# A hybrid encoder layer in fp32r: four more pairs of up tiles by seven products, their weight sums made in DRAM

## The chip, the cores and the metric

The kernel runs on one core of a Trainium2 chip. The metric is device time in microseconds (us). TensorE is called PE (its weight loads PEld), VectorE DVE, ScalarE ACT, GpSimd POOL, and SyncE SP, which issues most of the transfers.

## The reference

One layer on x (512 tokens by 1024 channels, float32) and a memory of 256 tokens:

```python
h = rmsnorm(x, norm_mix)
(fq, fk, fv, ff, gq, gk, gv, gb, ga, gz, sq, sk, sv, gates) = split_projection(h @ w_in)
ya = fox_attention(...)            # 4 heads, softmax with a forgetting gate
yb = gated_delta_rule(...)         # 4 heads, chunked recurrence
yc = stick_breaking_attention(...) # 4 heads, blocks of 128 queries, strict causal mask
mixed = g0 * (ya @ w_oa) + g1 * (yb @ w_ob) + g2 * (yc @ w_oc)
x = x + mixed @ w_out
x = x + memory_cross_attention(rmsnorm(x, norm_xq), rmsnorm(mem, norm_mem), w_mq, w_mkv, ..., w_mo)
x = x + conv_ffn(rmsnorm(x, norm_ffn), w_up, ffn_conv, ffn_conv_b, w_down)

def conv_ffn(h, w_up, conv_w, conv_b, w_down):
    u = causal_dwconv(h @ w_up, conv_w) + conv_b
    a, b = jnp.split(u, 2, axis=-1)
    return (jax.nn.silu(a) * b) @ w_down
```

w_up is 1024 by 5632, w_down 2816 by 1024. The last line of the layer, the gated MLP, is what the change is about.

## The kernel before, in words

Everything lies with channels on the 128 partitions and the 512 tokens along the row. Weights come in units of 128 x 1024 float32 (512 KB): eight blocks of 128 x 128. A matrix product is kept exact enough by splitting each float32 operand into a high part, rounded to the matmul's type fp32r, and a low part, the rest; a block then takes three matmuls: high by high, weight's high by the tokens' low, and weight's low by the tokens' high. `mm3` puts the 16 matmuls with the weight's high part first (L212, L213) and the 8 with its low part behind (L215).

A unit is loaded by SP into one of three raw tiles (`wraw`, L178), its high part copied by ACT (`whi`, L186), its low part subtracted by DVE (`wlo`, L187). `split_adding` makes the low part without DVE: ACT writes the negated, rounded weights into `alo` (L292), and a DMA issued by POOL adds the raw weights from DRAM to it (L293).

The program runs in stages: three mixers with their gates, in an order written out by hand (`ORDER`: a letter for a step, a number for a head or half); the output projection; the cross-attention; the up products, and the down products. Each engine then works through its own instructions in the order that the program and its scheduler gave it; a wait at the head of an engine's queue holds everything behind it. POOL has little to do: in each of the four stick-breaking heads (`s0` to `s3`) it writes the causal mask into score tiles (AFFINE_SELECT at L846 and L858), and later it issues the `alo` transfers. DVE and ACT wait for these masks, and the stick head is interleaved with the gate products on PE.

The up stage has 22 pairs m of tiles (tile m and tile m + 22: the two inputs of the gate). Three kinds of pairs:

- raw pairs (m below `RAW_UP`): the products start from the un-normalised tokens `xf`, while the root of the mean square, `r_f`, is still being made (`xfps`, `rfa`, `rfb`, L1050 to L1061); the results are multiplied by `r_f` (L1191);
- plain pairs: 48 matmuls of 512 columns on the normalised tokens `xn`, made by `up_norm` (L1078 to L1080);
- seven-product pairs (m in `SEVEN`): the pair of units and the tokens' halves taken as a 2 by 2 block product in seven half products instead of eight (`seven`, 84 matmuls of 256 columns). They need four sums of weight blocks a pair (s1 to s4, DVE, L305 to L315) and sums of the tokens, made once (`token_forms`).

`gated` then runs the convolution, the silu and the product, and gives `hid`. The down stage takes 12 of the 22 hidden tiles by seven products too (`seven_down`, with sums of four weight blocks a unit by DVE at L1247 to L1249) and the others plainly, in two halves of four output tiles.

Of the kernel before, what the change touches and what calls it, by code (L numbers as in the profile page):

```python
# [16 lines left out]
P = 128  # L17
# [5 lines left out]
SPARE = 2  # L23
JS = (5, 6, 7, 8, 9, 10)
FORM_SLOTS = 8
AHEAD = 4
ADD_A22 = True
ADD_PLAIN = (0, 1)
# [53 lines left out]
def build(nc, tc, ctx, x_t, mem_t, w, cols_d, const_d, unit_d, out_t, dbg=None):  # L82
# [9 lines left out]
    def tiles_of(which, tag, bufs, shape=(T,)):  # L92
# [19 lines left out]
    ahead = tiles_of("ahead", "a", AHEAD, (1024,))  # L112
# [5 lines left out]
    spilled = ctx.enter_context(tc.tile_pool(name="spill", bufs=1, space=bass.MemoryType.DRAM)).tile(  # L118
        [P, KC, T], F32, tag="x3", name="x3_spill")
# [54 lines left out]
    last_mm = []  # L174

    def load_unit(u):
        raw = wp.tile([P, 1024], F32, tag="wraw", name=f"wraw{u}", bufs=WB[0])
        nc.sync.dma_start(raw, w[u])  # L178
        return raw
# [101 lines left out]
    def sums_of_tokens(e, o, f):  # L281


        V.tensor_tensor(e[:, LEFT], e[:, RIGHT], e[:, LEFT], ALU.subtract)
        V.tensor_tensor(two(f), two(e), o[:, None, RIGHT].to_broadcast([P, 2, T // 2]), ALU.add)
        V.tensor_tensor(e[:, RIGHT], f[:, LEFT], o[:, LEFT], ALU.subtract)

    def split_adding(u, src, cols, name):

        lo = ahead(f"alo{name}", F32R)[:, :cols.stop - cols.start]  # L290
        hi = wp.tile([P, 1024], F32R, tag="whi", name=f"whi{name}", bufs=WB[1])[:, :cols.stop - cols.start]
        S.activation(lo, src, AF.Copy, scale=-1.0)  # L292
        G.dma_start(lo, w[u, :, cols], accum_op=ALU.add)  # L293
# [3 lines left out]
    def seven(u, name, xs, forms, sums, outs, rest):  # L297


        a1, a2 = load_unit(u), load_unit(u + 1)  # L300
        (a11, a12), (a21, a22) = [(t[:, :T], t[:, T:]) for t in (a1, a2)]

        h1, l1 = split_adding(u, a1, slice(0, 2 * T), f"{u}")
        s1, s2, f12 = sums("12")
        V.tensor_tensor(s1, a21, a22, ALU.subtract)  # L305
        V.tensor_tensor(s2, a11, s1, ALU.subtract)
        w5, w6 = f12()
        if ADD_A22:
            h2, l2 = split_adding(u + 1, a22, slice(T, 2 * T), f"{u + 1}")
        else:  # L310
            h2, l2 = (wp.tile([P, 1024], F32R, tag=t, name=f"{t}{u + 1}", bufs=b) for t, b in (("whi", WB[1]), ("wlo", WB[2])))
            split_blocks(a22, h2[:, :T], l2[:, :T])
# [1109 lines left out]
```

## Time and profile before

| | |
|---|---|
| median of 3 runs | 1044.39 us (1044.11 to 1044.57) |
| profiled execution's own time | 1044.74 us |
| its span | 1043.0 us |
| busy: PE, DVE, ACT, POOL | 1029.4, 748.8, 602.8, 58.1 us |
| moved by DMA | 115.06 MB, of it 14.42 MB by POOL's accumulates |
| up stage on PE | from 691.28 to about 923.4 us |
| granted TensorE clock | 1.00 |

A row of a timeline gives the start and length in us, engine, line, operation, output tile <- input tiles; a bracket tells how long the engine had been idle and what ended that. PE's instructions overlap a little, so the distance between starts (0.23 us for 512 columns, 0.12 for 256), not the length of one, is what a matmul costs.

### The profile page before, as it was taken

To read this page: it belongs to the slowest core of one execution; us is meant where nothing else is said; L and a number is where in the kernel's file an instruction comes from. 1 tells how busy PE (TensorE), PEld (TensorE's weight loads), DVE (VectorE), ACT (ScalarE), POOL (GpSimd) and SP (SyncE) were. 2 spreads that over 40 slices of the span, in tenths; PEclk is the share of its full clock that TensorE was granted. 3 is DMA by queue.
4 is the path that set the end of the run, shared out by engine and by line. 5 is a ranking of instruction groups with operands and counts; after the bars stand their busy time and mean duration, and the time that the engine had idled before them with its cause. 6 is when DMAs were issued, how large, how long until landed. Compare 5 with 4: busy or idle time off the path is not lost.

```text
span 1043.0 us, 14582 instructions
## 1 busy us (share of the span) xinstructions
PE 1029.4 (99%) x5529; PEld 873.1 (84%) x5529; DVE 748.8 (72%) x1262; ACT 602.8 (58%) x986; POOL 58.1 (6%) x116
## 2 busy tenths in 40 slices
PE   9999999999999999999999999999999999999998
PEld 7778888778888888788887888778889999989997
DVE  6697768788455443457657757679889988999873
ACT  6376757646242644654545657655677777855431
POOL 0000000101010000000000000000111111100000
PEclk9999999999999999999999999999999999999999
DMA  6323221111211111222434323142777788732441
GB/s 235 101 81 101 76 67 61 72 61 63 80 61 62 59 43 61 81 81 81 153 123 127 122 86 119 43 158 96 188 179 185 178 194 191 173 101 103 161 143 61
DMA packets 34342, 115.06 MB, mean 110 GB/s; under 512 B 3936, under 2 KB 4192, under 8 KB 33760
## 3 DMA queue, kind: packets, MB, share of 16 engines
q1 hardware_dynamic: 29088, 99.45, 28.3%
q0 software_dynamic: 4896, 14.42, 8.4%
q8 instruction: 43, 0.70, 0.3%
q10 hardware_dynamic: 288, 0.27, 0.1%
q14 instruction: 27, 0.22, 0.1%
HBM read 109.93 MB, written 4.19 MB: 109 GB/s over the span
## 4 chain that ended last, share of the span: by engine, by line
PE 94%; DVE 2%; ACT 1%; DMA 1%; issue 1%; SPq 0%; POOL 0%; ACTq 0%; DVEq 0%; POOLq 0%
PE dn L1221 8%; PE g L212 4%; PE g L213 4%; PE g L215 4%; PE up L215 3%; PE up L213 3%; PE up L212 3%; PE px L267 2%; PE px L269 2%; PE gk L469 2%; PE px L266 2%; PE dz L1221 2%; PE dx L1221 2%; PE f L212 1%; PE s L213 1%; PE s L215 1%
## 5 line engine op out<-in xcount | busy, mean ns | idle before, releaser
L186 ACT ACTIVATE whi<-wraw 128x1024 fp32r<-128x1024 f32 x117 | 123.8, 1058 | 150.4 <-PE g L213 38.7
L187 DVE TENSOR_TENSOR wlo<-wraw,whi 128x1024 fp32r<-128x1024 f32 x117 | 142.7, 1220 | 42.7 <-ACT whi L186 21.4
L212 PE MATMUL g<-hh,whi 128*128 128x512 f32 x192 | 77.5, 404 | 1.6 <-DVE gate L485 1.6
L213 PE MATMUL g<-hl,whi 128*128 128x512 f32 x192 | 75.8, 395 | 0.0
L293 POOL DMA_DIRECT2D alo<-w x34 | 29.5, 866 | 422.2 <-ACT alo L292 419.8
L215 PE MATMUL g<-hh,wlo 128*128 128x512 f32 x192 | 51.5, 400 | 0.0
L1221 PE MATMUL dn<-room,whi 128*128 128x256 f32 (+1 forms) x176 | 49.6, 333 | 0.0
L1118 DVE SCALAR_TENSOR_TENSOR uc<-u,cols,uc 128x511 f32<-128x511 f32 (+1 forms) x68 | 48.5, 749 | 0.7 <-ACT uc L1116 0.7
L212 PEld LDWEIGHTS g<-hh,whi 128*128 128x128 f32 x192 | 36.2, 188 | 10.8 <-DVE gate L485 1.4
L215 PEld LDWEIGHTS g<-hh,wlo 128*128 128x128 f32 x192 | 35.8, 188 | 8.3 <-issue 0.5
L213 PEld LDWEIGHTS g<-hl,whi 128*128 128x128 f32 x192 | 36.2, 188 | 7.7
L294 ACT ACTIVATE whi<-wraw 128x1024 fp32r<-128x1024 f32 (+1 forms) x34 | 30.3, 892 | 15.9 <-PE py L267 8.8
L485 DVE TENSOR_TENSOR gate<-g,r_x 128x512 f32<-128x512 f32 x24 | 16.4, 688 | 30.8 <-PE g L215 30.8
L292 ACT ACTIVATE alo<-wraw 128x1024 fp32r<-128x1024 f32 (+1 forms) x34 | 30.2, 887 | 13.1 <-DMA wraw<-w 12.1
L274 DVE TENSOR_TENSOR sl<-s,sh 128x1024 fp32r<-128x1024 f32 x26 | 31.8, 1223 | 5.2 <-ACT sh L273 5.1
L1221 PE MATMUL dn<-room,wlo 128*128 128x512 f32 (+1 forms) x128 | 34.0, 352 | 0.0
L1221 PEld LDWEIGHTS dn<-room,whi 128*128 128x128 f32 x176 | 29.8, 188 | 3.4
L212 PE MATMUL up<-xnh,whi 128*128 128x512 f32 x80 | 31.6, 395 | 0.0
L1221 PE MATMUL dn<-hidl,whi 128*128 128x512 f32 x80 | 31.6, 395 | 0.0
L213 PE MATMUL up<-xnl,whi 128*128 128x512 f32 x80 | 31.6, 395 | 0.0
L273 ACT ACTIVATE sh<-s 128x1024 fp32r<-128x1024 f32 x26 | 27.3, 1051 | 5.6 <-PE px L267 3.2
L1116 ACT ACTIVATE uc<-u,cols 128x512 f32<-128x512 f32 x34 | 26.7, 809 | 4.5 <-DVE u L1191 3.6
(991 smaller groups left out, 3094.4 us busy)
## 6 DMA issues: line engine op xcount, KB each, us to landing
wraw<-w SPq DMA_DIRECT2D x166, 512.0 KB, 3.5
alo<-w POOLq DMA_DIRECT2D x21, 512.0 KB, 6.4
alo<-w POOLq DMA_DIRECT2D x13, 256.0 KB, 5.8
x<-x_t SPq DMA_DIRECT2D x8, 256.0 KB, 6.7
xr<-x_t SPq DMA_DIRECT2D x2, 1024.0 KB, 5.9
x_spill<-xr SPq DMA_DIRECT2D x2, 1024.0 KB, 4.3
x<-x_spill SPq DMA_DIRECT2D x8, 256.0 KB, 4.1
mem_sb<-mem_t SPq DMA_DIRECT2D x4, 256.0 KB, 4.7
```

The costliest lines, as they stand in the source:

```text
L186: S.activation(hi, raw, AF.Copy)
L187: V.tensor_tensor(lo, raw, hi.bitcast(F32), ALU.subtract)
L212: PE.matmul(ps, hi[:, b], xh, start=first and i == 0, stop=False)
L213: PE.matmul(ps, hi[:, b], xl, start=False, stop=False)
L215: mm = PE.matmul(ps, lo[:, b], xh, start=False, stop=last and i == len(xs) - 1)
L273: S.activation(hi, src, AF.Copy)
L274: V.tensor_tensor(lo, src, hi.bitcast(F32), ALU.subtract)
L292: S.activation(lo, src, AF.Copy, scale=-1.0)
L293: G.dma_start(lo, w[u, :, cols], accum_op=ALU.add)
L294: S.activation(hi, src, AF.Copy)
L1118: V.scalar_tensor_tensor(c[:, s:], u[:, :T - s], col("ffn_conv", 3 * j + 2 - s), c[:, s:], ALU.mult, ALU.add)
L1221: mm = PE.matmul(ps[:, z], lhs, rhs, start=first is None, stop=last, skip_group_check=True)
```

## The change

`SEVEN` grows from 13 pairs to 17 (m = 5 to 21), `RAW_UP` from 4 to 5 (m = 0 to 4), so no normalised plain pair is left. Norms and token forms are made between the raw pairs (`TOKENS`), in place. All ten raw units use `split_adding`, with their low parts in tiles of the pool "hidden" (tags `wsh`, `wsl`); before, the raw units were split by DVE, and `alo` lay in a pool of its own ("ahead").

The sums of weights aren't made by DVE any more. For each seven-product pair SP copies two units within DRAM, and POOL issues three accumulating DMAs from DRAM to DRAM, one for a step of the program (`sums_of_weights`; 512 KB, 256 KB, 256 KB); for each three units of the down stage two copies and four accumulates (`sums_of_down`). `advance_sums` runs one step of every open job after the steps named in `SUMS_AFTER`, from `A0` on; POOL's DMAs are pinned in program order. `seven` and `seven_down` load the finished sums through SP and split them. The signs of the seven products change with that, the low parts of seven-product units are split by DVE, and the down stage's first half runs its plain blocks with the hidden tile outside and both pairs of outputs within each group of units.

```diff
+SUMS_AFTER = {s: 1 for s in "A0 C0 n0 S1 S2 s1 s2 n1 z n2 n3 S3 s3 a0 y0 A1 a1 B0 c0 y1 y2 C1 c1".split()}
+ADD_RAW = (0, 1)
-RAW_UP = 4
-FORMS = 4
-NORMS = {0: 2, 1: 6}
-SEVEN = (7, 8, 9, 10, 11, 12, 13, 14, 16, 17, 18, 19, 20)
-SPLITS = {18: 10}
+RAW_UP = 5
+FORMS = 3
+TOKENS = {0: "n0 n4 f0", 1: "n1 n5 f1", 2: "n2 n6 f2", 3: "n3 n7 f3"}
+SEVEN = (5, 6, 7, 8, 9, 10, 11, 12, 13, 14, 15, 16, 17, 18, 19, 20, 21)
+SPLITS = {18: 3, 19: 2, 20: 2}
...
-    def split_adding(u, src, cols, name):
-
-        lo = ahead(f"alo{name}", F32R)[:, :cols.stop - cols.start]
...
+    def split_adding(src, dram, name, alloc):
+
+        lo = alloc(f"alo{name}", F32R)
+        hi = wp.tile([P, 1024], F32R, tag="whi", name=f"whi{name}", bufs=WB[1])
         S.activation(lo, src, AF.Copy, scale=-1.0)
-        G.dma_start(lo, w[u, :, cols], accum_op=ALU.add)
+        G.dma_start(lo, dram, accum_op=ALU.add)
         S.activation(hi, src, AF.Copy)
         return hi, lo
...
+    def sums_of_weights(m):
+
+        u = UNITS["up"] + 2 * m
+        t = dram.tile([P, 2048], F32, tag=f"sums{m}", name=f"sums{m}")
+        s31, s2, s4 = t[:, :1024], t[:, 1024:1536], t[:, 1536:]
+        summed[m] = t
+        with tc.issue_after(last_load[0]):
+            nc.sync.dma_start(s31, w[u + 1])
+            nc.sync.dma_start(t[:, 1024:], w[u])
+        yield
+        pin(G.dma_start(s31.rearrange("p (a b) -> p a b", a=2), w[u:u + 2, :, :T].rearrange("a p b -> p a b"), accum_op=ALU.add))
+        yield
+        pin(G.dma_start(s2, s31[:, T:], accum_op=ALU.add))
+        yield
+        pin(G.dma_start(s4, s2, accum_op=ALU.add))
...
+    def advance_sums(n):
+
+        for s in list(steps):
+            if next(s, steps) is steps:
+                steps.remove(s)
+        for _ in range(n):
+            job = next(jobs, None)
+            if job is not None:
+                steps.append(job)
+                next(job)
...
+        h1, l1 = load("1", w[u])
+        hs31, ls31 = load("3", sums[:, :1024])
+        h2, l2 = load("2", w[u + 1, :, T:])
+        hs24, ls24 = load("4", sums[:, 1024:])
...
+        if name in SUMS_AFTER:
+            advance_sums(SUMS_AFTER[name])
...
+    def up_norm(k):
+
+        if not halves:
+            halves.extend(nquad(f"xn{z}{c}", F32R) for z in "hl" for c in (0, 4))
+        hi, lo = (halves[2 * z + k // 4][:, k % 4] for z in range(2))
+        t = x3[k]
+        V.scalar_tensor_tensor(t, t, col("norm_ffn", k), r_f, ALU.mult, ALU.mult)
+        z = LEFT if k < 4 and all(m in SEVEN for m in range(RAW_UP, NF)) else slice(0, T)
+        split_blocks(t[:, z], hi[:, z], lo[:, z])
...
-        if z in ADD_PLAIN and m > FORMS:
-            unit = split_adding(u, load_unit(u), slice(0, 2 * T), f"{u}")
+        if z in ADD_RAW and m < RAW_UP:
+            unit = split_adding(load_unit(u), w[u], f"{u}", (wsumh, wsuml)[z])
```

POOL in the stick-breaking heads. Before, from the last masks of head 2 (s221, s222) to those of head 3 (s320 and on):

```order
L858 AFFINE_SELECT s221_3053<-s221_3053 128x128 [waits Activation_49,Pool_49]
...
L858 AFFINE_SELECT s222_3051<-s222_3051 128x128 [waits Activation_49,Pool_49]
L846 AFFINE_SELECT s320_3492<-s320_3492 128x128 [waits DVE_49,PE_49]
L858 AFFINE_SELECT s320_3492<-s320_3492 128x128 [waits Activation_49]
L846 AFFINE_SELECT s321_3494<-s321_3494 128x128 [waits DVE_49,PE_49]
```

In the change the same place, its later part (`sums12` is the DRAM tile of pair 12; L311, L313, L315 are the first, second and third accumulate of a pair; DMASW counts POOL's own earlier transfers):

```order
L311 DMA sums11_3159<-w 128x2x512 [waits DMAHW3_49,DMASW1_49]
L315 DMA sums10_3072<-sums10_3072 128x512 [waits DMASW0_49]
L903 AFFINE_SELECT s320_3558<-s320_3558 128x128 [waits DVE_49,PE_49]
L313 DMA sums11_3159<-sums11_3159 128x512 [waits DMAHW4_49,DMASW1_49]
L311 DMA sums12_3207<-w 128x2x512 [waits DMAHW5_49,DMASW4_49]
L315 DMA sums11_3159<-sums11_3159 128x512 [waits DMASW3_49]
L313 DMA sums12_3207<-sums12_3207 128x512 [waits DMAHW6_49,DMASW4_49]
L311 DMA sums13_3350<-w 128x2x512 [waits DMAHW3_49,DMASW7_49]
L315 DMA sums12_3207<-sums12_3207 128x512 [waits DMASW6_49]
L915 AFFINE_SELECT s320_3558<-s320_3558 128x128 [waits Activation_49]
L313 DMA sums13_3350<-sums13_3350 128x512 [waits DMAHW4_49,DMASW7_49]
L311 DMA sums14_3398<-w 128x2x512 [waits DMAHW5_49,DMASW2_49]
```

Behind these stand one more accumulate (pair 13's last) and then the mask of s321. Ahead of them, since the last mask of head 2, stand five more accumulates, of pairs 8, 9 and 10. Where there were masks only, 16 transfers now stand between the last mask of head 2 and that of s321.

PE at the start of the up stage (up0 and up22 are pair 0's two products, up1 and up23 pair 1's; whi the high parts, wlo and alo the low ones). Before, up0 runs to its end, around the two matmuls of the summed squares, before up22 starts:

```order
L213 MATMUL up0_5920<-xfl4_5833,whi101_5923 128x512 [waits DVE_49]
L215 MATMUL up0_5920<-xfh0_5742,wlo101_5924 128x512 x4
L215 MATMUL up0_5920<-xfh4_5832,wlo101_5924 128x512
L350 MATMUL xfps_5899<-xfh_5900,ones_r_81 128x512 [waits Activation_49]
L215 MATMUL up0_5920<-xfh4_5832,wlo101_5924 128x512 x3
L351 MATMUL xfps_5899<-xfl_5901,ones_r_81 128x512 [waits DVE_49]
L212 MATMUL up22_5951<-xfh0_5742,whi102_5954 128x512
```

In the change, the rows from the summed squares on, with the repeating high products left out:

```order
L408 MATMUL xfps_6031<-xfh_6032,ones_r_81 128x512 [waits Activation_49]
L409 MATMUL xfps_6031<-xfl_6033,ones_r_81 128x512 [waits DVE_49]
L211 MATMUL up22_6084<-xfh0_5872,whi102_6088 128x512
...
L211 MATMUL up1_6154<-xfh0_5872,whi103_6158 128x512 [waits Activation_49]
...
L214 MATMUL up0_6052<-xfh0_5872,alo101_6055 128x512 [waits DMAHW4_49,DMAHW3_49,DMAHW5_49,DMASW3_49,DMAHW6_49,DVE_49,PE_49]
L214 MATMUL up0_6052<-xfh0_5872,alo101_6055 128x512 x3
L214 MATMUL up0_6052<-xfh4_5963,alo101_6055 128x512 x4
L211 MATMUL up23_6186<-xfh0_5872,whi104_6190 128x512 [waits Activation_49]
```

The low products of up0 have moved behind all high products of up0, up22 and up1, and wait for a DMA.

ACT in the change, from the root's steps on (before, whi104 stood right behind whi103 there):

```order
L1123 ACTIVATE rfb_6040<-rfa_6039 128x512 [waits Activation_49]
L294 ACTIVATE whi103_6158<-wraw103_6155 128x1024 [waits DMAHW5_49]
L292 ACTIVATE alo101_6055<-wraw101_6053 128x1024 [waits DVE_49,Activation_49]
L292 ACTIVATE alo102_6087<-wraw102_6085 128x1024
L292 ACTIVATE alo103_6157<-wraw103_6155 128x1024
L272 ACTIVATE xnh0_6131<-xr0_4790 128x256 [waits DVE_49] x2
...
L272 ACTIVATE xnh4_6132<-xr1_4792 128x512 [waits DVE_49]
L292 ACTIVATE alo104_6189<-wraw104_6187 128x1024 [waits DMAHW1_49]
L294 ACTIVATE whi104_6190<-wraw104_6187 128x1024 [waits PE_49]
```

The DVE event that alo101 waits for is the one that frees the pool's memory: r_f. Eight high parts of the normalised tokens stand between the copies and whi104.

More of the change, by code (lines that the diff above doesn't have):

```diff
@@ L294, in split_adding @@
         S.activation(hi, src, AF.Copy)
         return hi, lo
[L297 to L312, printed above, removed]
-        s3, s4, f34 = sums("34")
-        V.tensor_tensor(s3, a21, a11, ALU.subtract)
-        V.tensor_tensor(s4, a12, s2, ALU.subtract)
-        w7, w3 = f34()
+    summed, steps = {}, []
@@ new lines, in sums @@
+    def sums():
+        yield from (sums_of_weights(m) for m in SEVEN)
+        n = len(JS) // 2
+        plain = 2 * (NF // 2 - len(JS))
+        for first in (PLAIN_AT[0] // 8, (plain * 4 + PLAIN_AT[1]) // 8 + 2 * n):
+            yield from (sums_of_down([UNITS["down"] + first + n * i + k for k in range(n)]) for i in range(2))
+    summed_down, jobs = {}, sums()
+    def advance_sums(n):
[7 more added lines that the diff above has]
+                next(job)
@@ L1100, in seven_up @@
[L1100 to L1109 removed]
+    xn, halves, quarters = [None] * KC, [], []
```

234 lines of the change are left out of this document (121 added, 113 removed).

## The prediction

> **What bounds the kernel now.** I read the page's shares first, then a table by stage, then the chain of waits through the up products, and last the timelines of the two places where the change puts a new wait. From the page, the busy line and the chain by engine:
>
> ```profile
> PE 1029.4 (99%) x5529; PEld 873.1 (84%) x5529; DVE 748.8 (72%) x1262; ACT 602.8 (58%) x986; POOL 58.1 (6%) x116
> ...
> PE 94%; DVE 2%; ACT 1%; DMA 1%; issue 1%; SPq 0%; POOL 0%; ACTq 0%; DVEq 0%; POOLq 0%
> ```
>
> TensorE (PE) is busy 1029.4 of 1043.0 us. So only two things can move the time: fewer PE microseconds, or PE made to wait. The table by stage (columns: length, then busy time of PE, PEld, DVE, ACT, POOL, then clock, DMA share, GB/s):
>
> ```profile
> 400.00:450.00 50.00, 50.00 (x240) 40.85 (x240) 22.13 (x33) 26.08 (x46) 2.82 (x9) 1.00 0.22 74
> 690.00:735.00 45.00, 44.31 (x190) 35.33 (x189) 37.61 (x57) 24.86 (x33) 0.00 (x0) 1.00 0.32 110
> 771.00:851.00 80.00, 80.00 (x675) 79.95 (x674) 70.55 (x117) 62.22 (x84) 13.79 (x16) 1.00 0.79 186
> 952.00:993.00 41.00, 41.00 (x299) 38.75 (x298) 34.88 (x58) 17.57 (x22) 0.00 (x0) 1.00 0.42 142
> ```
>
> The seven-product stretch (771 to 851) has PE full, DVE at 70.55 of 80 and ACT at 62.22. Nothing there waits, so taking the weight sums off DVE buys nothing by itself. It only keeps the extra seven pairs from making DVE the bound.
>
> **The gain: four pairs.** A plain unit between seven pairs and the five seven pairs behind it, from the chain of waits (start, length, what):
>
> ```profile
> 851.15 0.23 PE up L212
> ...
> 862.32 0.12 PE px L263
> ...
> 912.26 0.23 PE up L212
> ```
>
> 851.15 to 862.32 is one plain pair, 11.17 us. 862.32 to 912.26 is five seven pairs, 49.94 us, so 9.99 each. The difference is 1.18 us a pair. Thirteen seven pairs become seventeen; a fifth raw pair takes the place of a normalised plain one at the same price. Four times 1.18 is **-4.7 us**. The down products have as many matmuls as before in another order, and 952 to 993 shows that stage full: 0, with up to 2 us lost if a split is late at the turn between its halves. DVE there is busy 34.88 of 41, and without the down sums it has less.
>
> **The raw stage.** All ten raw units now get their low part by a negative copy on ACT and an accumulating DMA from POOL. The tile that takes it lies in the pool "hidden", which opens only where the last reader of the cross stage is done, and the order shows ACT's first negative copy (alo101) behind DVE's r_f. On PE the high products of three units now stand ahead of that unit's low product. Before, in the timeline:
>
> ```profile
> 691.28 0.39 PE L212 MATMUL up<-xfh,whi 128*128 128x512 f32 x1
> 692.09 1.22 DVE L187 TENSOR_TENSOR wlo<-wraw,whi 128x1024 fp32r<-128x1024 f32 x1
> 694.62 0.50 PE L213 MATMUL up<-xfl,whi 128*128 128x512 f32 x1 [0.15 <-DVE xfl L205]
> 695.89 0.50 PE L213 MATMUL up<-xfl,whi 128*128 128x512 f32 x1 [0.53 <-DVE xfl L205]
> 698.31 0.40 PE L351 MATMUL xfps<-xfl,ones_r 128*128 128x512 f32 x1
> 701.51 0.69 DVE L1060 SCALAR_TENSOR_TENSOR rfa<-rfb,rfa 128x512 f32<-128x512 f32 x1
> 702.12 1.22 DVE L187 TENSOR_TENSOR wlo<-wraw,whi 128x1024 fp32r<-128x1024 f32 x1
> 703.26 0.42 DVE L1061 TENSOR_SCALAR r_f<-rfa 128x512 f32<-128x512 f32 x1
> 704.57 1.52 ACT L1116 ACTIVATE uc<-u,cols 128x512 f32<-128x512 f32 x2 [1.04 <-DVE u L1191]
> ```
>
> After: without the 1.22 us split at 692.09, DVE's xfl comes in time, and the two PE stalls of 0.15 and 0.53 us go; a wait of some 0.5 us for the summed squares (xfps), which no low product covers any more, comes in: **-0.2**. Sixteen matmuls at 0.23 us end at 695.0, the second xfps starts near 695.75 and PE goes on at 696.0. Two further high products (2 x 3.72) end at **703.4**: there PE wants alo101. From that xfps to r_f took 698.31 to 702.2, had DVE not put the split of 702.12 in between, then 0.42: 4.3 in all. So r_f is done near 700.1, ACT's copy (1.04) at 701.15, POOL issues at 701.2, and the tile is there one landing later. For the landing, the page's DMA issues, the answer on that tile, and the issues and queues between 735 and 771 us:
>
> ```profile
> wraw<-w SPq DMA_DIRECT2D x166, 512.0 KB, 3.5
> alo<-w POOLq DMA_DIRECT2D x21, 512.0 KB, 6.4
> alo<-w POOLq DMA_DIRECT2D x13, 256.0 KB, 5.8
> ...
> L293 POOL DMA_DIRECT2D alo<-w x34: 853/862/1013, 736.6 to 903.7; - x34
> ...
> DMA to landing us min/median/max: 4.7/6.0/8.3
> ...
> q0 software_dynamic: 892, 3.00, 49.8%
> ...
> wraw<-w SPq DMA_DIRECT2D x8, 512.0 KB, 4.8
> alo<-w POOLq DMA_DIRECT2D x6, 512.0 KB, 6.8
> ```
>
> Medians are 6.4 us for 512 KB (call it a) and 5.8 for 256 KB (b), all at a DMA share near 0.79. A plain load lands in 4.8 us there against 3.5 over the run, so company costs about 1.3 of it. At shares of 0.22 to 0.32, where the new ones run, that bounds a from below by 6.4 - 1.3 = 5.1 and b by 4.5; from above by 6.8 and 6.2. The new sums go from DRAM to DRAM in pieces of 2 KB, which no row shows, so I don't take the low end: a = 6.0, b = 5.4. Then alo101 lands at 707.2, **+3.8 us** (2.9 to 4.6). There is a floor beside it: behind the three copies ACT has eight high parts of the normalised tokens, each behind a DVE norm, and only then alo104 and whi104, which PE's next high product needs. Norms and splits between 700 and 735, and ACT's two copies:
>
> ```profile
> L1078 DVE SCALAR_TENSOR_TENSOR xn<-xr,cols,r_f 128x512 f32<-128x512 f32 x8 | 5.5, 749 | 0.0
> ...
> L292 ACT ACTIVATE alo<-wraw 128x1024 fp32r<-128x1024 f32 (+1 forms) x34 | 30.2, 887 | 13.1 <-DMA wraw<-w 12.1
> L294 ACT ACTIVATE whi<-wraw 128x1024 fp32r<-128x1024 f32 (+1 forms) x34 | 30.3, 892 | 15.9 <-PE py L267 8.8
> ```
>
> 700.1 + 5.5 + 0.6 + 1.04 + 1.05 = 708.3, against 703.4 + 1.87 where PE would come to it: 3.0. So landings shorter than 5 us save little here. The later alos are issued a unit or more ahead.
>
> The Trainium skill, page "DMA: Bandwidth & Descriptors", section "Anatomy of one DMA — SWDGE (gpsimd) path", fits such a DMA as 2.0 us plus its bytes over 436 thousand a microsecond, 3.2 us for 512 KB and 2.6 for 256 KB. The 6.4 and 5.8 above disagree. The same section says that a semaphore wait is taken on the issuing sequencer before dispatch, and by that POOL's later work stands behind each waiting sum.
>
> **POOL in the stick heads.** The DRAM sums are steps on POOL's queue, pinned in program order: each step's DMA waits for the landing of the one before of its pair. Between the last mask of head 2 and the masks of head 3 (s320, s321) there are now 7, 6 and 3 such DMAs. Before:
>
> ```profile
> 408.51 0.29 POOL L858 TENSOR_SCALAR_AFFINE_SELECT s<-s 128x128 f32<-128x128 f32 x1 [7.11 <-ACT s L857]
> 418.72 0.29 POOL L846 TENSOR_SCALAR_AFFINE_SELECT s<-s 128x128 f32<-128x128 f32 x1 [9.91 <-DVE s L845]
> 437.14 0.29 POOL L846 TENSOR_SCALAR_AFFINE_SELECT s<-s 128x128 f32<-128x128 f32 x1 [8.87 <-DVE s L845]
> ...
> 437.47 0.42 ACT L847 ACTIVATE s<-s 128x256 fp32r<-128x256 f32 x1 [1.80 <-POOL s L846]
> 438.75 0.49 ACT L842 ACTIVATE s<-sz 128x384 f32<-128x384 f32 x1 [0.86 <-PE sz L840]
> 439.21 1.06 ACT L186 ACTIVATE whi<-wraw 128x1024 fp32r<-128x1024 f32 x1
> ...
> 441.72 0.40 PE L212 MATMUL g<-hh,whi 128*128 128x512 f32 x1
> ```
>
> What is queued behind the mask of 437.14: ACT's exponential, a softplus step, and the weight split (whi) that PE needs at 441.72 for the next gate. Mask, 0.42, 0.46 and 1.06 leave it until 439.5 at the latest. POOL is free at 408.8 and issues one DMA in 0.87 us. Pair 10's 512 KB step is issued third, at 410.5; the 256 KB step behind it waits until 410.5 + a, and right behind that goes pair 11's 512 KB step, at 411.4 + a. So it goes on through pairs 12 and 13: pair 13's step is issued at 413.2 + 3a, the next one waits for its landing at 413.2 + 4a, the last waits b more, and s321 comes at 414.1 + 4a + b. With a = 6.0 and b = 5.4 that is 443.5: **+4.0 us**. At 5.1 and 4.5 it is 439.0, nothing; at 6.8 and 6.2, 447.5, +8.0. The wait is hidden as long as 4a + b is under 25.4. The mask at 418.72 comes at 411.4 + a + b = 422.8, about where its slack ends. The masks after s321 follow PE's shift. The steps of heads 1 and 2 stand in longer gaps, and those after 450 meet no POOL work until the raw stage.
>
> The copies for these sums go on SP between the weight loads, at most 4.7 MB (three jobs of 1.57) in one place. The queue that carries loads, and what ends the idle time ahead of the weight splits:
>
> ```profile
> q1 hardware_dynamic: 29088, 99.45, 28.3%
> ...
> L186 ACT ACTIVATE whi<-wraw 128x1024 fp32r<-128x1024 f32 x117 | 123.8, 1058 | 150.4 <-PE g L213 38.7
> ```
>
> 28.3% of 1043.0 us for 99.45 MB is 2.97 us a MB, so 4.7 MB pass in 14 us. The splits wait for PE to free their tiles, not for a load, and loads are three tiles ahead with a tile used every 5.6 us or more: 0, up to 3 us if one load in those places is late.
>
> **Sum.** Profiled run 1044.74 (span 1043.0 and 1.7 around it; 0.35 above the median of 1044.39). -4.7 - 0.2 + 3.8 + 4.0 = +2.9: **1047.6 us**.
>
> **Rivals.** *Only the raw stage waits* (landings near 5.1 and 4.5): POOL's masks are in time and the raw floor of 3.0 stays: 1044.74 - 4.7 - 0.2 + 3.0 = 1042.8, within 0.2%. The 4.7 of the fastest alo speaks for it, the 6.4 median against. By the Trainium skill's fit above ("DMA: Bandwidth & Descriptors") it would be this time too, since the floor stays. *Longer landings* (a 6.8, b 6.2, as between 735 and 771): 8.0 + 4.6 in waits, 1052.4; for it: a DRAM destination and 2-KB pieces, against it: little other traffic. *Faster*: the raw wait is not there, because r_f ends some 3 us before my 700.1 or the high products reach alo101 that much later in work, and the landings are short enough for the masks: 1044.74 - 4.9 = 1039.8, up to 1041.5 with part of the floor. It decides from a whi104 ready at 705.3. Against it: each link from xfps to whi104 has its row above, and ACT's queue is in order.
>
> **Numbers.** Both waits 0.50 (1045.5 to 1050.5), only the raw one 0.24, longer landings 0.12, faster 0.14. A change under 0.2% (2.1 us) can't be told from none: faster is under 1042.3, slower over 1046.5. From the first case 0.43 is slower and 0.07 same; the second is same but for 0.03; so faster 0.17, same 0.28, slower 0.55. The range, 1041.5 to 1053, takes in the second case and the longer landings.
>
> **What would show it.** In the changed profile: seven pairs at 10.0 us and PE busy some 4.7 us less; near 703 a PE wait of 3 to 5 us ahead of the first `up<-xfh,alo`, put down to a DMA or POOL; near 440 a PE wait of about 4 us ahead of a gate product, with ACT behind POOL's mask; landings of `sums` of 5.5 to 6.5 us. The prediction is wrong if those masks come before 439.5, if PE waits elsewhere (a late weight load in the gates, a split in the down stage), or if the seven pairs cost more than 10 us beside the loads of their sums.

## The result, and the profile after

| | before | after |
|---|---|---|
| median | 1044.25 us (1043.52 to 1044.57, 4 runs) | 1096.34 us (1093.3 to 1097.79, 4 runs) |
| profiled execution's own time | 1044.74 us | 1097.79 us |
| its span | 1043.0 us | 1096.1 us |
| busy: PE, DVE, ACT, POOL | 1029.4, 748.8, 602.8, 58.1 us | 1034.0, 737.9, 591.9, 103.6 us |

The change makes the kernel 5% slower: the ratio is 1.0496 (1.0476 to 1.0516). The forecast was 1047.6 us, with 1053 as its upper end.

From the page of the changed kernel: busy time, and the granted clock and the DMA share in 40 slices of 27.4 us, in tenths.

```profile
PE 1034.0 (94%) x5673; PEld 883.5 (81%) x5673; DVE 737.9 (67%) x1238; ACT 591.9 (54%) x978; POOL 103.6 (9%) x159
...
PEclk9999999999999999796999999998999999999999
DMA  6232212254599659999999832228845655562852
```

PE's share falls from 99 to 94%. The DMA engines are full in most of the slices 12 to 23, from 300 to 630 us. The granted clock drops in slices 17 and 19, among these, and in slice 28, where the raw stage begins. The view of PE's waits (the line that waits, what it waits for: us in all, times, longest) names four new ones; in the kernel before, the largest group was 1.6 us.

```profile
PE sz L906 <- ACT s L904: 20.6, 2, 16.1
PE g L211 <- ACT whi L185: 17.6, 1, 17.6
PE up L214 <- issue: 8.1, 1, 8.1
PE wo L211 <- ACT whi L185: 2.7, 1, 2.7
```

Together they are 49.0 of the 53.1 us by which the span grew. PE's busy time, which should have fallen by 4.7, rose by 4.6: behind these waits the granted clock is down for some us, as the point on the clock below works out.

**What fills the DMA engines.** The table by stage and the view of the DMA for 300 to 600 us, of the kernel before (first row) and of the changed one:

```profile
300.00:600.00 300.00, 298.21 (x1448) 245.00 (x1447) 170.67 (x270) 154.30 (x273) 11.21 (x30) 1.00 0.27 90
```

```profile
300.00:600.00 300.00, 260.87 (x1221) 212.10 (x1220) 139.08 (x214) 125.39 (x216) 73.78 (x94) 0.94 0.90 195
...
q0 software_dynamic: 13354, 21.61, 52.0%
q1 hardware_dynamic: 11248, 36.64, 38.1%
...
wraw<-w SPq DMA_DIRECT2D x36, 512.0 KB, 7.0
sums<-w POOLq DMA_DIRECT2D x17, 512.0 KB, 12.1
sums<-sums POOLq DMA_DIRECT2D x34, 256.0 KB, 7.2
sumsd<-w SPq DMA_DIRECT2D x8, 768.0 KB, 21.0
```

The share goes from 0.27 to 0.90. POOL's accumulates (q0) take 52.0% of all 16 engines for 21.61 MB, 7.2 us a MB, where SP's queue (q1) takes 3.1 us a MB. Landings are long there: 12.1 us for a sum's 512-KB step, 21.0 for a 768-KB copy of the down sums, 7.0 for a plain weight load, which took 3.5 over the whole run of the kernel before.

**The masks of head 3.** POOL's timeline (an issue, then in brackets how long POOL had been idle and what it waited for):

```profile
409.74 1.84 POOL L311 DMA_DIRECT2D sums<-w  x1
...
419.13 0.82 POOL L313 DMA_DIRECT2D sums<-sums  x1 [2.58 <-DMA sums<-w]
419.66 1.49 POOL L311 DMA_DIRECT2D sums<-w  x1
...
426.88 0.62 POOL L903 TENSOR_SCALAR_AFFINE_SELECT s<-s 128x128 f32<-128x128 f32 x1
432.01 0.85 POOL L313 DMA_DIRECT2D sums<-sums  x1 [4.51 <-DMA sums<-w]
...
458.31 0.84 POOL L313 DMA_DIRECT2D sums<-sums  x1 [4.91 <-DMA sums<-w]
...
463.44 0.85 POOL L315 DMA_DIRECT2D sums<-sums  x1 [3.08 <-DMA sums<-sums]
463.99 0.61 POOL L903 TENSOR_SCALAR_AFFINE_SELECT s<-s 128x128 f32<-128x128 f32 x1
```

The first mask comes at 426.9 instead of 418.7 and s321 at 464.0 instead of 437.1. Between the issue at 409.74 and the last mask stands the chain that the prediction wrote down. From the issue of a 512-KB step to POOL's next one, which waits for its landing, it is 9.4 us (409.74 to 419.13), 12.35 (419.66 to 432.01), then 9.8 and 15.4; the last 256-KB step takes 5.1. The 20.6 us of the list are two waits of PE: 4.5 us that end at 427.89, behind the mask of s320, and 16.1 us that end at 465.11, behind that of s321.

**A weight load behind the copies.** SP's timeline, and the chain of waits at the same place:

```profile
470.17 0.33 SPq L177 DMA_DIRECT2D wraw<-w  x1
470.56 1.77 SPq L326 DMA_DIRECT2D sumsd<-w  x1
...
477.94 6.68 SPq L326 DMA_DIRECT2D sumsd<-w  x1
484.66 5.24 SPq L327 DMA_DIRECT2D sumsd<-w  x1
490.00 3.01 SPq L177 DMA_DIRECT2D wraw<-w  x1
```

```profile
485.85 1.87 PE g L214 x8
...
490.00 25.43 DMA wraw<-w
...
516.90 0.79 PE g L211
```

Six 768-KB copies of the down sums go ahead of one load of a gate's weights. An issue on SP, 0.33 us for the load at 470.17, takes up to 6.7 us; the load behind the copies is issued at 490.0 and lands 25.4 us later. PE stands still for 17.6 us.

**The raw stage.** The same three steps as in the prediction, from the timelines of DVE, ACT, POOL and PE:

```profile
745.73 0.43 DVE L1126 TENSOR_SCALAR r_f<-rfa 128x512 f32<-128x512 f32 x1
746.26 2.96 ACT L292 ACTIVATE alo<-wraw 128x1024 fp32r<-128x1024 f32 x3 [1.05 <-DVE r_f L1126]
747.87 2.67 POOL L293 DMA_DIRECT2D alo<-w  x3 [129.49 <-ACT alo L292]
...
757.75 3.75 PE L214 MATMUL up<-xfh,alo 128*128 128x512 f32 x8 [8.11 <-issue]
```

POOL issues at 747.87, PE goes on at 757.75: 9.9 us from the issue to the first product that reads the tile. The eight products then take 3.75 us, where the eight at 485.85 above took 1.87.

**The pairs.** The first product of two seven pairs, eight pairs apart, in PE's timeline:

```profile
883.48 0.28 PE L262 MATMUL px<-xnh,whi 128*128 128x256 f32 x1
...
963.43 0.28 PE L262 MATMUL px<-xnh,whi 128*128 128x256 f32 x1
```

79.95 us for eight pairs, 9.99 each, as forecast.

### The profile page after: what moved, and what is told of

The parts are those of the page before. It is cut to its first block, busy times and chain, and to the rows that moved or that the text cites. A ratio compares the mean times of both kernels' runs of the same rounds, so it can differ in the third digit from the quotient of the medians.

```text
span 1096.1 us, 15108 instructions
## 1 busy us (share of the span) xinstructions
PE 1034.0 (94%) x5673; PEld 883.5 (81%) x5673; DVE 737.9 (67%) x1238; ACT 591.9 (54%) x978; POOL 103.6 (9%) x159
## 4 chain that ended last, share of the span: by engine, by line
PE 85%; DMA 5%; DVE 3%; issue 3%; ACT 3%; POOL 1%; SPq 0%; POOLq 0%; ACTq 0%; DVEq 0%
PE dn L1270 7%; PE g L211 4%; PE g L212 4%; DMA wraw<-w 3%; PE g L214 3%; PE px L266 3%; PE px L268 3%; PE px L265 2%; PE gk L526 2%; PE up L214 2%; PE dz L1270 2%; PE dx L1270 2%; PE f L211 1%; PE py L266 1%; PE py L268 1%
## 5 line engine op out<-in xcount | busy, mean ns | idle before, releaser
L185 ACT ACTIVATE whi<-wraw 128x1024 fp32r<-128x1024 f32 x107 | 113.2, 1058 | 155.2 <-PE g L212 37.6
L186 DVE TENSOR_TENSOR wlo<-wraw,whi 128x1024 fp32r<-128x1024 f32 x107 | 130.4, 1219 | 59.5 <-ACT whi L185 37.2
L211 PE MATMUL g<-hh,whi 128*128 128x512 f32 x192 | 79.2, 412 | 19.2 <-ACT whi L185 17.6
L1168 DVE SCALAR_TENSOR_TENSOR uc<-u,cols,uc 128x511 f32<-128x511 f32 (+1 forms) x88 | 62.5, 744 | 0.4 <-ACT uc L1166 0.4
L272 ACT ACTIVATE whi<-wraw 128x1024 fp32r<-128x1024 f32 (+2 forms) x46 | 38.7, 840 | 38.7 <-PE dn L1270 20.9
L1270 PE MATMUL dn<-room,whi 128*128 128x512 f32 (+1 forms) x256 | 58.5, 353 | 0.2 <-ACT whi L185 0.2
L273 DVE TENSOR_TENSOR wlo<-wraw,whi 128x1024 fp32r<-128x1024 f32 (+2 forms) x46 | 43.8, 955 | 19.9 <-ACT whi L272 13.1
L272 ACT ACTIVATE sh<-s 128x1024 fp32r<-128x1024 f32 x34 | 36.1, 1060 | 38.8 <-PE px L266 35.9
L1270 PEld LDWEIGHTS dn<-room,whi 128*128 128x128 f32 x256 | 44.6, 188 | 7.4 <-ACT whi L185 0.4
L266 PE MATMUL px<-xnl,whi 128*128 128x256 f32 x136 | 33.6, 281 | 0.0
L211 PE MATMUL up<-xfh,whi 128*128 128x512 f32 x80 | 31.9, 398 | 0.0
L212 PE MATMUL up<-xfl,whi 128*128 128x512 f32 x80 | 31.8, 397 | 0.0
## 6 DMA issues: line engine op xcount, KB each, us to landing
sums<-w POOLq DMA_DIRECT2D x17, 512.0 KB, 12.1
```

Of the source, the lines that this page charges most:

```text
L185: S.activation(hi, raw, AF.Copy)
L186: V.tensor_tensor(lo, raw, hi.bitcast(F32), ALU.subtract)
L211: PE.matmul(ps, hi[:, b], xh, start=first and i == 0, stop=False)
L212: PE.matmul(ps, hi[:, b], xl, start=False, stop=False)
L266: PE.matmul(ps, wh[:, block(i)], xl, start=False, stop=False, skip_group_check=not new)
L272: S.activation(hi, src, AF.Copy)
```

## Experiments

Where the quoted expectations name theories by letters, A is that the transfers of the sums make the new waits; the others stand for rivals in which the new order costs by itself. Unless said otherwise the diffs are against the changed kernel. Runs of the kernel before beside these gave medians from 1043.85 to 1044.49 us.

### Without the sums

**e1.** Nothing is copied or added in DRAM; `seven` and `seven_down` load plain weights in the place of the sums.

```diff
-        t = dram.tile([P, 2048], F32, tag=f"sums{m}", name=f"sums{m}")
...
+        summed[m] = (w[u + 1], w[u])
         yield
-        pin(G.dma_start(s31.rearrange("p (a b) -> p a b", a=2), w[u:u + 2, :, :T].rearrange("a p b -> p a b"), accum_op=ALU.add))
...
```

> The changed kernel with all sums in DRAM left out: no copies, no accumulates on POOL; the tiles of sums are loaded from the plain weights instead, so every later load and product is there but the up and down products of these units are not the reference's. Theory A (the sums' traffic and their steps on POOL cause the waits of 20.6 us at the stick head's masks, 17.6 and 2.7 us at weight splits, and some 7 of the 9.3 us of slower clock behind them): what is left is the four pairs' gain of 4.7 and the raw stage's wait of 8.1 with 2 us of slow clock, 1044.3 - 4.7 + 10 = 1049 to 1051 us. Rival B (the waits come from what else moved: loads of sums, the order of splits, POOL's place in the raw stage): over 1075 us.

Measured: 1050.61 us (1050.44 to 1050.78). So 45.7 of the 52 us belong to making the sums. PE's one new wait is the raw stage's:

```profile
PE up L214 <- issue: 8.3, 1, 8.3
```

It is as long as in the changed kernel, though no sum is made: the sums' traffic has no part in the long raw landing.

**e2.** The copies stay, the accumulates go.

```diff
         yield
-        pin(G.dma_start(s2, s31[:, T:], accum_op=ALU.add))
         yield
-        pin(G.dma_start(s4, s2, accum_op=ALU.add))
...
```

> The changed kernel with SP's copies kept and POOL's accumulates left out (sums are plain copies, so the products are not the reference's). If POOL's steps and their share of the DMA engines are the cause (theory A1): the masks are in time, the copies alone take some 24 MB at 3 us a MB, and weight loads wait little: 1049 to 1055 us. If weight loads are late because they stand behind the copies in SP's queue (A2): the waits of 17.6 and 2.7 us stay with their slow clock, 1070 to 1075 us.

Measured: 1051.29 us. With 24.1 MB of copies alone the time is 0.7 us above e1's, less than the 2.9 us by which executions of the kernel before differed beside these runs; between 300 and 600 us the share is 0.44, and the waits for weight splits are gone. It takes the accumulates to fill the engines.

**e4.** No sums, and all ten raw units split by DVE (`ADD_RAW = ()`), so that the raw landing is gone too.

```diff
-ADD_RAW = (0, 1)
+ADD_RAW = ()
```

> As the run without sums, and the ten raw units split by ACT and DVE as before the change instead of by copy and accumulate. If the raw stage's wait is the accumulate that can't start before r_f (theory A): that wait and its slow clock go too, and the four pairs' gain shows alone: 1044.3 - 4.7 = 1039 to 1041 us. If the wait is due to the norms and token forms made between raw pairs (rival C): 1045 us or more.

Measured: 1048.36 us (1047.47 to 1050.24), not the 1039 to 1041 that my theory had. With ten splits more, DVE is late with the tokens' forms at the start of the seven pairs, and waits of 0.8 to 1.1 us, stand close together; the granted clock is 0.83 between 750 and 770 us:

```profile
PE px L266 <- DVE t14l L273: 2.0, 2, 1.1
```

So the raw stage is tight on both sides: with the first units by POOL PE waits for a landing, and with none by POOL it waits for DVE.

**e5.** No sums, and the raw low parts by POOL only from the third pair on, where a landing has time.

```diff
-        if z in ADD_RAW and m < RAW_UP:
+        if z in ADD_RAW and 2 <= m < RAW_UP:
```

> As the run without sums (same computation left out), but the first two raw pairs split by ACT and DVE and only the later three by copy and accumulate. Theory A' (two separate costs in the raw stage: an accumulate that can't start before r_f, 8.3 us with slow clock behind it, and DVE too busy for the token forms if it splits all ten units, 3.6 us of waits with slow clock): the accumulates of the third pair on have time and DVE has six splits fewer, so neither is left: 1039 to 1042 us, the four pairs' gain of 4.7 alone. Rival C (norms and forms between raw pairs are late in any case): 1045 us or more.

Measured: 1041.53 us (1041.1 to 1042.25, 7 runs), ratio 0.9971 (0.996 to 0.9982). The 8.3-us wait is gone. This leaves the sums out and so is no solution, but it is what four more seven pairs and the new down order are worth when nothing waits. PE's busy time there:

```profile
PE 1025.8 (99%) x5673; PEld 877.5 (84%) x5673; DVE 741.4 (71%) x1242; ACT 588.0 (57%) x974; POOL 34.0 (3%) x88
```

3.6 us less than before, against the 4.7 forecast. By the starts of the stages in the two traces, PE enters the up stage 1.2 us earlier (690.05 instead of 691.28), is through it in 228.1 us instead of 232.0, and spends 121.2 instead of 119.7 on the down stage, with as many matmuls and columns as before: -1.2, -3.9 and +1.5.

### One part of the sums at a time

**e6.** All sums, but no step of them from n1 to S3, which keeps them out from between the masks of head 3; the steps that this leaves over follow behind.

```diff
-SUMS_AFTER = {s: 1 for s in "A0 C0 n0 S1 S2 s1 s2 n1 z n2 n3 S3 s3 a0 y0 A1 a1 B0 c0 y1 y2 C1 c1".split()}
+SUMS_AFTER = {'A0': 1, 'C0': 1, 'n0': 1, 'S1': 1, 'S2': 1, 's1': 1, 's2': 1, 's3': 1, 'a0': 1, 'y0': 1, 'A1': 1, 'a1': 1, 'B0': 1, 'c0': 1, 'y1': 1, 'y2': 1, 'C1': 1, 'c1': 1, 'B1': 1, 'y3': 1, 'b0': 1, 'b1': 0}
```

> The whole computation, one job of sums for each step as in the change, but no step of a sum from n1 to S3, so that no accumulate stands between the last mask of head 2 and the masks of head 3; the jobs left out there follow after head 3. Theory A (two costs: POOL's steps ahead of the masks, 20.6 us, and weight loads late in a full DMA system, 17.6 and 2.7): the masks' waits go, late loads stay: 1070 to 1080 us. Rival (DMA engines too full is all there is, and the masks' waits only stand in for it): PE waits as long elsewhere, 1088 us or more.

Measured: 1075.94 us (1073.4 to 1078.5), 20.4 less. The mask waits are gone; the weight loads behind the copies are not, only at another place:

```profile
PE wob L211 <- ACT whi L185: 16.9, 3, 9.5
```

**e7.** The change as it is, with the down sums made by DVE (as before) and their four jobs in DRAM left out.

```diff
-        for first in (PLAIN_AT[0] // 8, (plain * 4 + PLAIN_AT[1]) // 8 + 2 * n):
-            yield from (sums_of_down([UNITS["down"] + first + n * i + k for k in range(n)]) for i in range(2))
...
-        nc.sync.dma_start(t, summed_down[u])
+        V.tensor_tensor(d4[:, :2], d[:, 1:3], d[:, 0:1].to_broadcast([P, 2, 256]), ALU.add)
...
```

> The whole computation: the change as it is, but the down units' sums made by DVE, so that the copies of 4.7 MB and their accumulates are gone and all else of the up pairs' sums stays. If the wait of 17.6 us at a weight split is the load that stands behind those copies in SP's queue: it goes with 1.4 us of slow clock, masks' waits of 20.6 and the raw stage's 8 stay: 1074 to 1080 us. If it is the fullness of the DMA engines through the up pairs' accumulates: loads stay late by some 10 us or more, 1085 us or more.

Measured: 1077.78 us, 18.6 less. The other half this time: the 17.6 is gone and the masks' wait stays.

```profile
PE sz L904 <- ACT s L902: 19.7, 2, 15.0
```

With the copies but no accumulates (e2) no weight split makes PE wait, and with the up pairs' accumulates but no down copies (e7, at a share of 0.81 between 450 and 500 us) the longest such wait is 0.6 us. So the 17.6 us take both, the copies ahead of the load in SP's queue and the accumulates that hold the engines meanwhile.

**e8.** The change with e5's edit alone (raw low parts by POOL from the third pair on).

> The whole computation: the change as it is, but the first two raw pairs split by ACT and DVE. Only the raw stage's wait of 8.1 us and the 2 us of slow clock behind it should go: 1096 - 10 = 1085 to 1088 us. If that wait only took up lateness that shows elsewhere: over 1091 us.

Measured: 1091.23 us (1090.31 to 1092.16), 5.1 less, and not the 8.1 of wait and 2 of slow clock that my number went by (e1 and e5 differ by 9.1). It lies at the bound of the rival, over 1091, by which lateness shows elsewhere. The wait of 8.1 is gone, but the weight load's grew by 3.1 in this run, and the masks' from 20.6 to 21.1:

```profile
PE g L211 <- ACT whi L185: 20.7, 1, 20.7
```

Why it grew is open. Nothing that e8 changes comes before 735 us, so I take it for the spread of that wait: the changed kernel's own four times differ by 4.5 us. No run tests it.

### The sums placed otherwise

Four kernels make all sums in DRAM, or all those of the up pairs, with the steps spread more thinly. The table `SUMS_AFTER` names the steps at which a new job starts (1) and at which open ones only go on (0); both now run on through the output projection and the cross-attention, and the loop that emptied all jobs at the end of the cross stage is replaced by that:

```diff
-    advance_sums(NF + 4)
-    while steps:
-        advance_sums(0)
+        advance_sums(SUMS_AFTER.get("x" + step, 0))
```

**f2.** New jobs at A0, C0, n0 and S1, then at every second step from a0 on, none between S2 and S3; the down jobs in the raw and first seven pairs; raw units split by DVE.

> The whole computation: the changed kernel with raw units split by DVE, and the sums' jobs started at half the rate or less: four until S1, none until head 3 is over, then one for every second step of the program, the down units' in the first up pairs. Theory A (too much traffic at once, and POOL's steps ahead of masks): no wait of POOL or of a weight load over 2 us, 1040 to 1045 us. Rival (any sums in DRAM beside the weight loads make these late): 1050 to 1070 us.

Measured: 1058.27 us (1056.15 to 1062.08), ratio 1.0139 (1.011 to 1.0168): inside the rival's 1050 to 1070. No wait over 0.9 us is left in the gates. The down jobs' traffic now meets the start of the seven pairs, where a weight split waits for a late load; the second row below is DVE's late token forms, as in e4. PE's waits, and the table by stage for that stretch:

```profile
PE px L263 <- ACT whi L273: 4.5, 1, 4.5
PE px L266 <- ACT t14h L273: 2.8, 1, 2.8
...
740.00:770.00 30.00, 20.49 (x90) 16.87 (x89) 20.87 (x36) 11.10 (x17) 5.17 (x5) 0.85 0.94 200
```

**f3.** The other way: up and down jobs one in every third step, from F0 (the first step) through the cross stage; e5's raw edit.

> The whole computation: raw units as in the run with the first two pairs split by DVE, sums' jobs started one for every third step of the program from the first forgetting head to the end of the cross-attention, so that one job is under way at a time and all have landed before the up stage. Theory A: the same traffic over 600 instead of 300 us leaves the DMA engines near 0.65 busy, weight loads in time, POOL's steps landed when the next comes: 1040 to 1045 us. Rival (an accumulate of 8 to 12 us ahead of a mask or of POOL's work for the delta rule is enough to stop PE): 1048 us or more.

Measured: 1055.10 us (1054.47 to 1055.68), ratio 1.0102 (1.0087 to 1.0117): the rival's side. The head's masks still come late, though the engines aren't full: their share is 0.48 between 300 and 400 us. Waits of PE, and landings between 300 and 400 us:

```profile
PE sz L907 <- ACT s L905: 4.6, 1, 4.6
...
wraw<-w SPq DMA_DIRECT2D x11, 512.0 KB, 4.1
...
sums<-sums POOLq DMA_DIRECT2D x7, 256.0 KB, 4.7
sums<-w POOLq DMA_DIRECT2D x3, 512.0 KB, 8.7
```

This is the price that the prediction needed: at that share, with a plain load at 4.1 us, a 512-KB step from DRAM to DRAM lands in 8.7 us (7.7 between 200 and 300 us), above the 6.8 that I had as the upper bound; the 256-KB step, at 4.7, lies inside its bounds.

**f4.** f2's places for the 17 up jobs, the down sums by DVE, e5's raw edit.

> The whole computation: the run with spread sums (jobs four until S1, none until head 3 is over, then one for every second step), with two things changed: the first two raw pairs split by DVE and the later three by copy and accumulate, and the down units' sums made by DVE again, so that nothing is made in DRAM once the up stage begins. The run without sums gives 1041.5; in the spread run no PE wait over 0.7 us stood before the up stage. Theory A: 1041 to 1044 us, the change's gain without its waits. Rival (sums in DRAM cost PE something even when no wait is long, or DVE's down sums are late): 1046 us or more.

Measured: 1047.97 us median of 12 runs from 1042.29 to 1051.96, ratio 1.0032 (1.0016 to 1.0049): the median is on the rival's side, the fastest on that of A. The profiled execution, the fastest of them, has no PE wait over 1.6 us at a DMA share of 0.93 between 500 and 600 us. I take it that with the engines that full a load is late in some executions and not in others; the slower ones left no trace, so this is argued, not shown.

**f5.** As f4, thinner: jobs at F0, p0, A0, C0, n0, S1, then at every third step to the end of the cross stage.

> The whole computation: as the run with spread sums and DVE's down sums, whose times lay between 1042 and 1052 us with the DMA engines 0.9 to 1.0 busy from 500 to 700 us. Here the seventeen jobs are thinner: two in the first forgetting head, four until S1, then one for every third step until the end of the cross-attention. If the spread of times comes from weight loads that are now and then late in full DMA engines (theory A), the times draw together at 1041 to 1043.5 us. If it comes from elsewhere (POOL's steps, the start of the up stage), they stay spread up to 1050 us, or a wait shows at a mask.

Measured: 1044.12 us (1042.71 to 1046.51, 11 runs), ratio 0.9998 (0.9989 to 1.0008): as the kernel before. The spread is 3.8 us instead of 9.7, with the share down to 0.81 between 500 and 600 us:

```profile
500.00:600.00 100.00, 99.61 (x477) 82.25 (x476) 69.84 (x108) 54.24 (x90) 13.64 (x15) 1.00 0.81 219
```

The spread is now near the 3.2 us of the kernel before, which goes with the theory that f4's spread came from full engines; but the median is above the 1041 to 1043.5 that this theory had. It is the best kernel that makes the whole layer with the sums in DRAM, and it gains nothing.

### The sums made elsewhere

**h1** (against the kernel before). Can DVE make the sums of two more seven pairs?

```diff
-SEVEN = (7, 8, 9, 10, 11, 12, 13, 14, 16, 17, 18, 19, 20)
+SEVEN = (7, 8, 9, 10, 11, 12, 13, 14, 15, 16, 17, 18, 19, 20, 21)
```

> The kernel before, with pairs 15 and 21 by seven products too (15 instead of 13), sums by DVE as before: nothing in DRAM. If PE bounds: two pairs' gain, 1044.2 - 2.4 = 1041.9 us. If DVE bounds the end of the up stage (it is busy 11.00 of 11 us there while pair 21 runs plainly): the splits for the down stage come late, 1043 to 1048 us.

Measured: 1055.72 us (1054.64 to 1057.03), worse than either number. PE waits three times in the seven pairs, for ACT's split of a sum:

```profile
PE px L263 <- ACT sh L273: 5.1, 3, 2.6
```

What is late behind ACT is not settled. In the trace each of these splits stands on ACT behind a negative copy (`alo`) that waits for a weight load, and the first of these loads was issued at 865.36, when ACT's own high copy freed its raw tile. DVE is busy 42.24 of the 50 us from 850 on, less than the 45.05 in the kernel before. So fifteen pairs with the sums on DVE don't work as they stand, but that DVE's time is the limit isn't shown; the raw tiles and ACT's queue are at least as likely.

**i1, i2.** POOL makes the sums in SBUF from the raw tiles, by tensor adds; no DRAM sums at all. i1 has e5's raw edit, i2 has all raw units split by DVE.

```diff
-        hs31, ls31 = load("3", sums[:, :1024])
+        G.tensor_tensor(s31[:, :T], r2[:, :T], r1[:, :T], ALU.add)
+        G.tensor_tensor(s31[:, T:], r2[:, T:], r2[:, :T], ALU.add)
...
```

> The whole computation without any sum in DRAM: seventeen pairs by seven products, the four sums of a pair (and those of a down unit) made in SBUF by POOL's own adds from the raw tiles; the first two raw pairs split by ACT and DVE, the later three by copy and accumulate. POOL's add of 128x512 takes 1.04 us in the profile of before, so 4.2 us a pair of 10. If the change's loss is all in the traffic and steps of the sums, and the run without sums (1041.5) shows what is left: 1041 to 1043 us, 0.1 to 0.3% under before. Rival (adds on POOL slow DVE's work beside them, which is busy 8.9 of 10 us a pair, or the raw tiles are held too long): waits of PE ahead of px or py, 1046 us or more.

> As the run with POOL's adds, but all ten raw units split by ACT and DVE. From the run without sums and with these splits (1048.4, token forms 3.6 us late on DVE and PE slow behind it): 1047 to 1050 us. If the forms were late there only through chance: 1041 to 1043 us.

Measured: 1094.80 us (1094.17 to 1095.83) and 1102.56 (1101.96 to 1104.13); i1 falls on the rival's side, and i2 misses by as much. The rival had two reasons, adds that slow DVE's work and raw tiles that are held too long, and both show. For the first, in the groups of i1 between 750 and 900 us, a POOL add and two kinds of DVE operation beside it; behind them the same DVE operations of e5, where POOL adds nothing:

```profile
L360 POOL TENSOR_TENSOR s<-wraw,wraw 128x512 f32<-128x512 f32 x12 | 22.3, 1859 | 73.1 <-DMA wraw<-w 66.8 <-DVE uc L1161 6.3
...
L1171 DVE TENSOR_TENSOR hid<-uc,uc 128x512 f32<-128x512 f32 x8 | 9.9, 1234 | 0.0
...
L382 DVE TENSOR_TENSOR u<-py,u 128x256 f32<-128x256 f32 x8 | 3.4, 420 | 0.2
```

```profile
L1160 DVE TENSOR_TENSOR hid<-uc,uc 128x512 f32<-128x512 f32 x10 | 6.8, 684 | 0.0
L371 DVE TENSOR_TENSOR u<-py,u 128x256 f32<-128x256 f32 x10 | 4.2, 417 | 0.0
```

A DVE operation with both inputs in SBUF goes from 684 to 1234 ns; one that takes an input from PSUM stays at 417 to 420. The Trainium skill, page "SBUF — State Buffer", section "Who interferes with whom", says that a DVE instruction with two SBUF inputs contends with a GpSimd instruction that reads SBUF; these rows agree. For the second, between 800 and 900 us POOL waits 38.8 us for weight loads, at a DMA share of no more than 0.27, and SP stands 68.2 us waiting for DVE to be done with raw tiles before it issues the next load. DVE is busy 49.1 of the 50 us from 850 on, so the held tiles may follow from its slower work; no run parts the two.

## Why the prediction was wrong

The direction was right, the size far off: +52.1 us instead of +3.2 above the median, outside the range. By its steps:

- **The gain.** -4.7 was forecast for four seven pairs. The pairs cost 9.99 us, as forecast. The down stage lost 1.5 by e5, inside the 0 to 2 that were allowed and not counted in the sum; PE came to the up stage 1.2 us earlier in e5, a term that the prediction did not have. With all three e5 is 3.6 busy us lower.
- **POOL in the stick heads: the mechanism held, the landing a was mis-sized.** The order of the landings on POOL and what stands behind the mask on ACT (the exponential, then the weight split) came as written. PE stopped at the head's own product (sz, L906), which reads that exponential, and not at a gate product behind the split. With the measured steps from issue to issue (mean 11.74 for a, 5.13 for b) the prediction's formula 414.1 + 4a + b gives 466.2 for s321; it came at 463.99, as the first issue came 0.8 us earlier and an issue took 0.53 instead of 0.9. But a was taken as 6.0, and 6.8 at most. What failed is the step "At shares of 0.22 to 0.32, where the new ones run": that is the share of the kernel before, without the change's own transfers. In the changed kernel it is 0.90. At a share of 0.48 f3 still has 8.7 us, so part of the error is the price of such a step itself. The mask of s320, which the prediction put at 422.8, about where its slack ends, came at 426.9 and cost 4.5 us that had no term. Worth 20.4 us by e6, where 4.0 stood in the sum.
- **The sum that would have shown it** stood in the prediction's own rows. Between 735 and 771 us accumulates took 49.8% of 36 us for 3.00 MB, 6.0 us a MB; loads took 2.97. The change copies 24.1 MB (34 units of 512 KB, 8 pieces of 768 KB) and adds as many: 24.1 x (3.0 + 6.0) = 217 us of all 16 engines. Between 300 and 600 us fall 15.2 MB of the copies and 21.6 MB of the accumulates: by these prices 45.6 + 129.6 = 175 of 300 us, a share of 0.58 on top of 0.27. That is 0.85, where 0.90 was measured. The rows were used for how long one transfer takes, and not for how much there is.
- **The late weight load: bounded at 3 us, measured at 17.6.** The step was "4.7 MB pass in 14 us", which gives SP's queue all 16 engines. q0 held 59.0% of them and q1 moved 4.98 MB in the 50 us from 450 on: at that rate 4.7 MB take 47 us. The first of the copies was issued at 470.6, and the load behind them landed at 515.4, 44.8 us later. The DMA view of 450 to 500 us:

```profile
q0 software_dynamic: 2117, 3.96, 59.0%
q1 hardware_dynamic: 2360, 4.98, 33.8%
```

  The prediction had named this place as one that would make it wrong. Worth 18.6 us by e7.
- **The raw stage: order and times right, the landing too short.** From the stage's first product (737.86) to POOL's issue was 10.0 us, forecast 9.9; PE was ready for alo101 at 11.8, forecast 12.1. The landing was 9.9 us instead of 6.0, in e1 too, so the sums have no part in it. Three such DMAs are issued within 2.7 us there, where the row of before that priced them is of single ones. At 6.0 us a MB three of them are 9.4 us of all engines, with raw loads beside; that this is the cause is worked out, not tried apart. Wait forecast 3.8, measured 8.1.
- **No price for the clock.** Behind each of these waits PE's matmuls start 0.43 us apart instead of 0.23, for 3.0 to 4.6 us, and each costs 1.4 to 2.3 us more, whether the wait was 2.7 or 17.6 us; the granted clock is 0.61 in 516 to 521 us and 0.57 in 757 to 763. Five waits add up to some 8 us: 1034.0 busy us against e5's 1025.8. So the span grew by 49.0 of waits, 8.2 of slow clock and -3.6 of gain, 53.6 where 53.1 were measured. The Trainium skill, page "TensorE: Matmul & The Clock Gate", section "Part 1: The HAM clock gate (the "warmup" mystery)", has PE at half its clock after an idle window of some 3.4 us and back after as long a busy one. The 3.0 to 4.6 us fit the second; for the first, waits of 2.7 us here and of 2.3 in e8 were enough. Length alone doesn't decide it: 2.1 us in e6 and 2.8 in i1 were not followed by it, and waits of 0.8 to 1.1 us close together in e4 were.
- **The rival "longer landings"** (1052.4) had the right term and stopped at the durations of the trace of before. Its reasons, a DRAM destination and 2-KB pieces, are borne out as far as f3's 8.7 us at a share of 0.48 goes; "little other traffic", which was held against it, is what failed.

## What to carry to other kernels

Before pricing a moved transfer by its landing time, add up the engine time of all transfers that the change adds, by kind (us of 16 engines a MB), over the stretch where they run, and add that to the share already there; at the 0.90 of this case no landing of the old trace held. Then ask which queue carries loads that a compute engine waits for, and keep bulk copies out from ahead of them. In these runs a wait of PE of some 2.3 us or more mostly cost its length and 1.4 to 2.3 us of slow clock behind it, so several short ones can cost more than one long one of the same sum.

## What the runs showed of the hardware

- An accumulating DMA takes 7.2 us of all 16 engines a MB from DRAM to DRAM at a share of 0.90 (6.9 in f3 at 0.48), and 6.0 to SBUF, against 3.0 to 3.4 for a copy or a load. The Trainium skill, page "DMA: Bandwidth & Descriptors", section "Anatomy of one DMA — SWDGE (gpsimd) path", has a fit that gives 3.2 us for 512 KB. The traces disagree for accumulating ones: 8.7 us were measured at a share of 0.48 and 12.1 at 0.90.
- SP's issue of a copy of 768 KB takes up to 6.68 us at a DMA share of 0.93 (450 to 500 us), where that of a plain load takes 0.33.
- DVE and POOL slow each other: an add on POOL of 128 x 512 takes 1.86 us instead of 1.04 in the kernel before, and the DVE product beside it 1.23 instead of 0.68, as averages over operations that overlap and others that don't.
